# A two-layer backbone with 32 experts per layer: experts without split operands, and two gathers moved behind a loop

## The chip, the cores and the metric

The kernel runs on one core of a Trainium2 chip. The metric is the device time of one execution in microseconds; the time of a kernel is the median of its runs. The engines are TensorE (PE; its weight loads are listed as PEld), VectorE (DVE), ScalarE (ACT), GpSimd (POOL) and SyncE (SP), and 16 DMA engines serve the core.

## The reference

Two layers work on 512 latent rows and 256 context rows of 1024 floats. Each layer is a trunk (modulated norm, four mixers, output projection) and a mixture of experts over the rows; the second layer's mixture has only the 512 latent rows. All is fp32. The mixture, cut to what matters:

```python
def hier_moe(h, w_grp, b_grp, w_exp, b_exp, w_gate, w_up, w_down):
    ...  # group by the largest group logit, two experts inside it: gates, expert_id
    def expert_block(args):
        xb, e = args
        return (jax.nn.silu(xb @ w_gate[e]) * (xb @ w_up[e])) @ w_down[e]
    y_buf = lax.map(expert_block, (x_buf, blk_expert)).reshape(cap, d)
    ...
    y = y_buf[dest].reshape(n_tok, TOP_K_INNER, d).astype(jnp.float32) * gates[..., None]
    return jnp.sum(y, axis=1).astype(h.dtype)
```

A row goes to 2 of 32 experts. An expert has gate and up weights of 1024 x 512 and down weights of 512 x 1024: 2.1 MB each, 6.29 MB in all.

## The kernel before

Both layers run trunk, route, experts, in that order. The route ranks the experts by their number of rows; rank r has a fixed width `CAP[l][r]` of 24 to 128 rows, and what exceeds the widths goes through an overflow loop (`overflow`, a `For_i` at L1550 with a count that is read on the chip). Ranks 0 and 1 are fixed experts, whose weights are loaded during the route. The others are known only after it: SP reads the expert's number into a register and issues the loads of its weights with it (L148, by way of `unit2`).

**Slots.** Weights lie in slots of one unit, 128 x 1024 floats or 0.5 MB. Gate, up and down take four units each. `self.slots` holds 24 slots: a ring of 6 (`u`) and the halves of 9 double tiles (`xa`, `xb`, `xc`). Two neighbouring free slots of one double tile are filled by one load of 1 MB, others by two of 0.5 MB. `load()` issues the next loads in order as long as enough slots are free; it is called after every stage. Near the end of a layer, at the last split, the eight tiles of the split ring join the slots.

**Stages.** `seq` is the order of the products: gate (`g`), up (`u`) or both at once (`gu`) of expert e, then down (`d`) of expert e - 1. Three forms exist by width W:

- W over 64 ("many"): each unit is split into `hi` (a copy rounded to fp32r on ACT, L170) and `lo` (the difference, on DVE, L176) in rings of four tiles each, and every product is three fp32r passes on the full array (`mm3`, L195 to L197). The rows and the hidden part are split likewise. The unit's slot is given back after its split (`prep`, `done_with`), one stage ahead of the product.
- W of 33 to 64 (`gate_up2` L1403, `down2` L1458): plain fp32 in two column tiles of 64 of the array ("halves"), gate on one and up on the other.
- W up to 32 (`gate_up4` L1426, `down4` L1448): plain fp32 in four column tiles of 32 ("quarters").

In both of the last the slots are given back after the product. `rows` (L1382) transposes an expert's rows, `hT`, `hT1` and `hT4` the hidden part. `order` interleaves wide and narrow experts by `COST`; the four last ranks come at the end, and their result is added through a small product per 128 rows (`tailw`, L1839) and not scattered.

**Head of the expert stretch.** After the route POOL issues three gathers of rows (L1744, into three buffers `xb`), then a small memset that holds back the first splits (`mk`, L1757 to L1762), then the overflow loop follows, and behind it `rows(0)` and the loads of the dynamic experts.

**Widths in their order before.** Layer 0: 96 96 32 128 128 64 64 128 64 56 104 56 96 56 56 80 56 80 48 48 80 48 80 48 48 72 40 72 and four of 32. Layer 1: 96 96 32 32 96 32 96 32 88 24 80 24 72 24 72 24 72 56 56 48 48, six of 40, 72 and four of 32. So layer 0 has four experts over 96 rows, nine of 65 to 96, fourteen of 33 to 64 and five of up to 32; layer 1 has none, ten, ten and twelve.

Of the kernel before, what the change touches and what calls it, by code (L numbers as in the profile page):

```python
# [17 lines left out]
D = 1024  # L18
# [40 lines left out]
XU = ((6, 4, 8), (6, 10, 2))  # L59
# [5 lines left out]

QW = 32

COST = (19, 13, 8)
# [27 lines left out]
class K:  # L96
# [1276 lines left out]
    def xt_tile(self, l, mp, i):  # L1373
        return mp.tile([128, max(D, 8 * max(CAP[l]))], F32R, tag=f"XT{i}", name=self.nm("XT"), bufs=2)

    def rows(self, l, mp, X, W, few):
# [6 lines left out]
        v = ps.rearrange("p (k n) -> p k n", k=8)[:, :, 0:W]  # L1383
        xt = [self.xt_tile(l, mp, i)[:, 0:8 * W].rearrange("p (k t) -> p k t", k=8) for i in range(1 if few else 2)]
        if few:
            xt = xt[0].bitcast(F32)
            nc.vector.tensor_copy(xt, v)  # L1387
        else:
            nc.scalar.activation(xt[0], v, AF.Copy)
            nc.vector.tensor_sub(xt[1], v, xt[0].bitcast(F32))  # L1390
        return xt

    def halves(self, W):

        ps = self.pss("halves")
        return [ps[64 * j:64 * j + W, :] for j in range(2)]

    def gate_up2(self, xt, wg, wu):
        ps = self.halves(xt.shape[2])
        for k in range(8):  # L1400
            for j, w in enumerate((wg, wu)):
                n = w[0].shape[1]
                self.nc.tensor.matmul(ps[j], xt[:, k, :], w[k // n][:, k % n, :], start=(k == 0), stop=(k == 7),  # L1403
                                      tile_position=(0, 64 * j))
        return ps

    def hT1(self, mp, h):
        nc = self.nc
        W = h.shape[0]
        pt = self.pss("hT")  # L1410
        hv = h.rearrange("p (f k) -> p f k", k=4)
        for k in range(4):
            nc.tensor.transpose(pt[:, k * W:(k + 1) * W], hv[:, :, k], self.ident[0:W, 0:W])
        o = mp.tile([128, 2 * FE], F32R, tag="ey", name=self.nm("ehT"), bufs=3).bitcast(F32)[:, 0:4 * W]
        nc.vector.tensor_copy(o, pt[:, 0:4 * W])
        return o.rearrange("p (k t) -> p k t", k=4)

    def gate_up4(self, xt, wg, wu):

        ps = self.pss("quarters")[:, 0:256]  # L1420
        for k in range(8):
            for j, w in enumerate((wg, wu)):
                n = w[0].shape[1]
                for i in range(2):
                    a = 64 * j + 32 * i
                    self.nc.tensor.matmul(ps[a:a + 32, :], xt[:, k, :], w[k // n][:, k % n, 256 * i:256 * i + 256],  # L1426
                                          start=(k == 0), stop=(k == 7), tile_position=(0, a))
        return ps[0:64, :], ps[64:128, :]

    def hT4(self, mp, h):  # L1430
        nc = self.nc
        pt = self.pss("hT")[0:64, 0:256]
        hv = h.rearrange("p (f k) -> p f k", k=4)
        for k in range(4):
            nc.tensor.transpose(pt[:, k * 64:(k + 1) * 64], hv[:, :, k], self.ident[0:64, 0:64])
        o = mp.tile([128, 2 * FE], F32R, tag="ey", name=self.nm("ehT"), bufs=3).bitcast(F32)[:, 0:128]
        o = o.rearrange("p (k t) -> p k t", k=4)
        pv = pt.rearrange("p (k i t) -> p k i t", k=4, i=2)
        for i in range(2):
            nc.vector.tensor_copy(o[64 * i:64 * i + 64], pv[:, :, i, :])  # L1440
        return o

    def down4(self, ht, ws):
        ps = self.pss("quarters")[:, 0:256]
        for k in range(4):
            n = ws[0].shape[1]
            for j in range(4):
                self.lastm = self.nc.tensor.matmul(ps[32 * j:32 * j + 32, :], ht[:, k, :],  # L1448
                                                   ws[k // n][:, k % n, 256 * j:256 * j + 256], start=(k == 0),
                                                   stop=(k == 3), tile_position=(0, 32 * j))  # L1450
        return [ps[32 * j:32 * j + 32, :] for j in range(4)]

    def down2(self, ht, ws):
        py = self.halves(ht.shape[2])
        for k in range(4):
            n = ws[0].shape[1]
            for j in range(2):
                self.lastm = self.nc.tensor.matmul(py[j], ht[:, k, :], ws[k // n][:, k % n, j * 512:(j + 1) * 512],  # L1458
                                                   start=(k == 0), stop=(k == 3), tile_position=(0, 64 * j))
        return py  # L1460

    def gate_up(self, xt, ws):
        W = xt[0].shape[2]
        ps = self.pss("gate_up")
        for k in range(8):
            self.mm3(ps[0:W, :], (xt[0][:, k, :], xt[1][:, k, :]), self.row(ws, k), k == 0, k == 7)
        return ps[0:W, :]

    def hidden(self, mp, pg):
        h = mp.tile([128, FE], F32, tag="eh", name=self.nm("eh"), bufs=2)[0:pg.shape[0], 0:pg.shape[1]]  # L1470
        self.lasta = self.nc.scalar.activation(h, pg, AF.Silu)  # L1471
        return h

    def hT(self, mp, h):
        nc = self.nc
        W = h.shape[0]
        pt = self.pss("hT")
        hv = h.rearrange("p (f k) -> p f k", k=4)
        for k in range(4):
            nc.tensor.transpose(pt[:, k * W:(k + 1) * W], hv[:, :, k], self.ident[0:W, 0:W])  # L1480
        o = mp.tile([128, 2 * FE], F32R, tag="ey", name=self.nm("ehT"), bufs=3)
        f = [o[:, i * FE:i * FE + 4 * W] for i in range(2)]
        ht = [x.rearrange("p (k t) -> p k t", k=4) for x in f]
        nc.scalar.activation(f[0], pt[:, 0:4 * W], AF.Copy)
        nc.vector.tensor_sub(f[1], pt[:, 0:4 * W], f[0].bitcast(F32))
        return ht

    def down(self, ht, ws):
        W = ht[0].shape[2]
        py = [self.pss("down") for _ in range(2)]  # L1490
        for k in range(4):
            for n in range(2):
                self.mm3(py[n][0:W, :], (ht[0][:, k, :], ht[1][:, k, :]),
                         [x[:, n * 512:(n + 1) * 512] for x in self.row(ws, k)], k == 0, k == 3)
        return [p[0:W, :] for p in py]

    def rows_out(self, mp, py, g2, W):

        y = mp.tile([128, D], F32, tag="ey", name=self.nm("ey"), bufs=3)[0:W, :]
        n = D // len(py)  # L1500
        for i, (p, a) in enumerate(py):
            c = slice(i * n, (i + 1) * n)
            if g2 is None:
                self.nc.scalar.copy(y[:, c], p[0:W, :])  # L1504
            else:
                self.nc.vector.tensor_mul(y[:, c], p[0:W, :], g2[a:a + W, c])
        return y

    def tail_rows(self, py, j, Gs, Yr):

        a = slice(32 * j, 32 * j + 32)
        for n, (p, _) in enumerate(py):
            c = slice(n * 256, (n + 1) * 256)
            self.lastv = self.nc.vector.tensor_mul(Yr[a, c], p, Gs[a, c])
# [18 lines left out]
    def overflow(self, l, R, src, pp, mp):  # L1533
# [5 lines left out]
        raw, o, X, om = (self.xt_tile(l, mp, i % 2).bitcast(F32)[:, 0:D] for i in range(4))  # L1539
# [87 lines left out]
    def moe(self, l):  # L1627
# [23 lines left out]
        F0 = next(r for r in range(NE) if CAP[l][r] <= HW)  # L1651
        many, few = list(range(2, F0)), list(range(F0, NE))
        order = [0, 1]
        last = few[-NTL:]
        todo = [many, [r for r in few[:-NTL] if CAP[l][r] > QW], [r for r in few[:-NTL] if CAP[l][r] <= QW]]
        mean = sum(COST[i] * len(x) for i, x in enumerate(todo)) / (NE - 2 - NTL)
        ahead = COST[0] - mean
        while any(todo):
            i = next(i for i in ((2, 1, 0) if ahead > 0 else (0, 1, 2)) if todo[i])
            order.append(todo[i].pop(0))  # L1660
            ahead += COST[i] - mean
        order += last
        cap = [CAP[l][r] for r in order]
        few = [w <= HW for w in cap]
        tiny = [w <= QW for w in cap]

        seq = [("g", 0), ("u", 0)]
# [86 lines left out]
        for e in range(3):  # L1754
            gather(e)
# [249 lines left out]
```

## Time and profile before

| | us |
|---|---|
| median of 3 runs | 1918.69 |
| lowest to highest | 1917.55 to 1920.36 |
| profiled execution | 1926.93 |
| its span in the trace | 1925.1 |

The profiled execution is one more execution, with the profiler on. Times in the trace count from the start of its span. The expert stretch of layer 0 runs from about 484 to 1050 us, that of layer 1 from about 1376 to the end. A DMA share is the mean busy share of the 16 DMA engines in a stretch, PEclk the granted clock of TensorE as a share of its full 2.4 GHz; 0.50 is 1.2 GHz.

### The profile page before, as it was taken

What the parts mean: (1) busy time and instruction counts of PE and PEld (TensorE: products, weight loads), DVE (VectorE), ACT (ScalarE), POOL (GpSimd) and SP (SyncE); (2) the same over time, 40 slices, a digit from 0 to 9 for tenths busy, and PEclk for the clock granted to TensorE, in tenths of its full rate; (3) what the DMA queues carried; (4) which work ended last, traced back from release to release, by engine and by line L of the source; (5) the groups of instructions that cost most, each with busy time, mean ns of one, the idle gap of its engine ahead of it and who ended that gap; (6) DMA issues with size and microseconds to landing.
All of it is one profiled execution on the core that took longest, in us unless ns stands there. A gap on an engine that the chain in (4) does not pass through costs nothing.

```text
span 1925.1 us, 29963 instructions
## 1 busy us (share of the span) xinstructions
PE 1721.4 (89%) x11336; PEld 1113.1 (58%) x11336; DVE 1019.4 (53%) x1776; ACT 741.8 (39%) x1097; POOL 260.4 (14%) x271
## 2 busy tenths in 40 slices
PE   6999999997799999999985999999599888988866
PEld 3788688876575444444442788777466554433331
DVE  3666366546773453443526665764576565422325
ACT  4443364323573343342522564732354443200211
POOL 1000100123111111010010001011322111110010
PEclk9999999998799999999986999999699898999986
DMA  8358865453899999999997324336499999999995
GB/s 310 95 195 280 277 231 188 163 203 154 277 394 382 385 394 391 396 397 386 390 351 300 118 74 148 102 117 259 140 339 377 398 405 396 404 399 403 417 414 222
DMA packets 159605, 561.71 MB, mean 292 GB/s; under 512 B 19810, under 2 KB 46498, under 8 KB 123744
## 3 DMA queue, kind: packets, MB, share of 16 engines
q1 hardware_dynamic: 133840, 499.67, 68.8%
q0 software_dynamic: 21440, 54.16, 8.1%
q10 hardware_dynamic: 4176, 5.91, 0.9%
q8 instruction: 91, 1.49, 0.3%
q14 instruction: 58, 0.48, 0.1%
HBM read 533.54 MB, written 35.52 MB: 296 GB/s over the span
## 4 chain that ended last, share of the span: by engine, by line
DMA 26%; PE 18%; DVE 3%; issue 2%; ACT 1%; POOL 1%; SPq 0%; DVEq 0%; ACTq 0%; POOLq 0%
DMA u<-in_w_up 6%; DMA xb<-in_w_up 4%; DMA xb<-in_w_down 3%; DMA xb<-in_w_gate 3%; DMA u<-in_w_down 2%; DMA xa<-in_w_down 2%; PE zunits L195 2%; PE zunits L196 2%; PE zunits L197 2%; DMA h2d<-h 2%; PE quarters L1426 1%; DMA xa<-in_w_up 1%; PE tailw L1839 1%; PE transP L839 1%; DMA u<-in_w_gate 1%
## 5 line engine op out<-in xcount | busy, mean ns | idle before, releaser
L196 PE MATMUL gate_up<-lo,XT 128*96 128x512 f32 (+5 forms) x368 | 151.5, 412 | 7.6 <-DVE lo L176 7.2
L195 PE MATMUL gate_up<-hi,XT 128*96 128x512 f32 (+5 forms) x368 | 150.1, 408 | 8.9 <-ACT hi L170 8.1
L176 DVE TENSOR_TENSOR lo<-u,hi 128x1024 fp32r<-128x1024 f32 (+1 forms) x100 | 121.2, 1219 | 59.5 <-ACT hi L170 56.4
L197 PE MATMUL gate_up<-hi,XT 128*96 128x512 f32 (+5 forms) x368 | 149.2, 405 | 2.1 <-DVE XT L1390 2.1
L170 ACT ACTIVATE hi<-u 128x1024 fp32r<-128x1024 f32 (+1 forms) x102 | 105.6, 1044 | 106.1 <-PE zunits L196 52.3
L195 PE MATMUL zunits<-hT,hi 128*128 128x512 f32 (+1 forms) x384 | 140.3, 366 | 0.9 <-ACT cqs L689 0.8
L196 PE MATMUL zunits<-hT,hi 128*128 128x512 f32 (+1 forms) x384 | 136.2, 355 | 0.1
L1744 POOL DMA_INDIRECT xb<-h2d,tok x64 | 68.8, 1076 | 493.1 <-PE xTw L1382 468.4
L197 PE MATMUL zunits<-hT,lo 128*128 128x512 f32 (+1 forms) x384 | 135.3, 352 | 0.0
L176 DVE TENSOR_TENSOR lo<-xb,hi 128x1024 fp32r<-128x1024 f32 x100 | 118.6, 1221 | 25.1 <-ACT hi L170 24.1
L1810 POOL DMA_INDIRECT yd<-ey,dst x56 | 71.1, 1270 | 351.8 <-ACT ey L1504 171.7
L176 DVE TENSOR_TENSOR lo<-xa,hi 128x1024 fp32r<-128x1024 f32 x86 | 101.8, 1220 | 27.2 <-ACT hi L170 26.4
L170 ACT ACTIVATE hi<-xb 128x1024 fp32r<-128x1024 f32 x100 | 101.9, 1053 | 32.0 <-PE gate_up L197 28.6
L1387 DVE COPY XT<-xTw 128x256 f32<-128x256 f32 (+4 forms) x41 | 20.9, 511 | 173.5 <-PE halves L1403 105.9
L170 ACT ACTIVATE hi<-xa 128x1024 fp32r<-128x1024 f32 x86 | 87.5, 1053 | 32.0 <-DMA xa<-in_w_down 11.0
L1382 PEld LDWEIGHTS xTw<-cpack,xb 32*128 32x128 f32 (+10 forms) x512 | 64.1, 201 | 60.6 <-issue 26.7
L1382 PE MATMUL xTw<-cpack,xb 32*128 32x32 f32 (+10 forms) x512 | 72.0, 283 | 26.8 <-DVEq L1550 8.2
L1471 ACT ACTIVATE eh<-halves 56x512 f32<-56x512 f32 (+3 forms) x24 | 14.2, 591 | 207.0 <-PE halves L1403 207.0
L196 PE MATMUL down<-lo,ehT 128*96 128x512 f32 (+5 forms) x184 | 80.5, 437 | 7.3 <-DVE lo L176 6.7
L195 PE MATMUL down<-hi,ehT 128*96 128x512 f32 (+5 forms) x184 | 70.4, 444 | 16.1 <-ACT hi L170 16.1
L195 PEld LDWEIGHTS gate_up<-hi,XT 128*96 128x96 f32 (+5 forms) x368 | 59.8, 163 | 42.8 <-ACT hi L170 12.7
L196 PEld LDWEIGHTS gate_up<-lo,XT 128*96 128x96 f32 (+5 forms) x368 | 59.7, 162 | 42.6 <-DVE lo L176 17.2
(441 smaller groups left out, 3740.1 us busy)
## 6 DMA issues: line engine op xcount, KB each, us to landing
xb<-in_w_down SPq DMA_DIRECT2D x52, 1024.0 KB
xb<-in_w_up SPq DMA_DIRECT2D x50, 1024.0 KB
u<-in_w_ada SPq DMA_DIRECT2D x96, 512.0 KB
u<-in_w_up SPq DMA_DIRECT2D x91, 512.0 KB
xa<-in_w_down SPq DMA_DIRECT2D x40, 1024.0 KB
xb<-in_w_gate SPq DMA_DIRECT2D x36, 1024.0 KB
xa<-in_w_gate SPq DMA_DIRECT2D x35, 1024.0 KB
u<-in_w_gate SPq DMA_DIRECT2D x58, 512.0 KB
```

What stands on the lines that cost most here:

```text
L170: self.nc.scalar.activation(h, v, AF.Copy)
L176: self.nc.vector.tensor_sub(o, v, h.bitcast(F32))
L195: mm(out, a[0], b[0], start=start, stop=False)
L196: mm(out, a[0], b[1], start=False, stop=False)
L197: self.lastm = mm(out, a[1], b[0], start=False, stop=stop)
L839: nc.tensor.transpose(ps[:, c - a:c - a + 128], p[:, c:c + 128], self.ident)
L1382: nc.tensor.transpose(ps[:, k * 128:k * 128 + W], Xv[:, :, k], self.ident[0:W, 0:W])
L1387: nc.vector.tensor_copy(xt, v)
L1426: self.nc.tensor.matmul(ps[a:a + 32, :], xt[:, k, :], w[k // n][:, k % n, 256 * i:256 * i + 256], start=(k == 0), stop=(k == 7), tile_posi ...
L1744: self.lastp = nc.gpsimd.indirect_dma_start(out=X[e][0:cap[e], :], out_offset=None, in_=self.h2d[l][:, :], in_offset=bass.IndirectOffsetOn ...
L1810: nc.gpsimd.indirect_dma_start(out=self.yd[l][:, :], in_=y, in_offset=None, out_offset=bass.IndirectOffsetOnAxis(ap=R["dst"][0:cap[e], ord ...
L1839: nc.tensor.matmul(ps[:, c], self.G[:, t * 128:(t + 1) * 128], Yr[:, c], start=True, stop=True)
```

## The change

- No operand of an expert is split. `parts(W)` gives the parts of the rows: up to 32 one on quarters, 33 to 64 one on halves, 65 to 96 one of 64 on halves and one of 32 on quarters, 97 to 128 two of 64 on halves. `products` runs, for each k, the matmuls of all parts in turn: two for a part on halves, four for one on quarters. All are plain fp32.
- The eight `hi`/`lo` tiles are slots from the start, and since the second row tile (`XT`) goes there is room for ten double tiles instead of nine: 6 + 20 + 8 = 34 slots.
- Gate and up of every expert are loaded together (eight units), and slots are given back only after the product.
- One gather stands ahead of the overflow loop; gathers 1 and 2 follow it. The overflow takes the buffers of gathers 1 and 2 for two of its tiles. The memset, the hold and `prep` go.
- `COST` has four classes, and the order is made anew. Layer 0: 96 96 32 128 64 64 128 64 56 56 128 56 56 104 56 48 48 96 48 80 48 80 48 80 40 80 72 72 and four of 32. Layer 1: 96 96 32 32 32 96 32 96 24 88 24 80 24 72 24 72 56 56 48 48, six of 40, 72 72 and four of 32.

```diff
-XU = ((6, 4, 8), (6, 10, 2))
+XU = ((6, 4, 10), (6, 10, 4))
...
-COST = (19, 13, 8)
+COST = (24, 19, 13, 8)
...
+    def parts(W):
+
+        n = -(-W // QW)
+        return {1: [(0, QW)], 2: [(0, W)], 3: [(0, HW), (HW, QW)], 4: [(0, HW), (HW, HW)]}[n]
+
+    def streams(self, ps, n, w, ws):
+
+
+        m = 2 if w > QW else 4
+        c = n // m
+        o = []
+        for j in range(m):
+            b = 128 // m * j
+            x, f = divmod(c * j, n // len(ws))
+            o.append((ps[b:b + w, 0:c], b, ws[x], slice(f, f + c)))
+        return o
+
+    def products(self, x, parts, ws, n, K, name):
+
+
+        S, out = [], []
+        for a, w in parts:
+            ps = self.pss(name)
+            st = self.streams(ps, n, w, ws)
+            S += [(a, w) + y for y in st]
+            out.append((ps, [y[0] for y in st]))
+        for k in range(K):
+            for a, w, o, b, m, c in S:
+                q = m[0].shape[1]
+                self.lastm = self.nc.tensor.matmul(o, x[:, k, a:a + w], m[k // q][:, k % q, c], start=(k == 0),
+                                                   stop=(k == K - 1), tile_position=(0, b))
+        return out
+
+    def gate_up(self, mp, xt, parts, wg, wu):
+
+
         nc = self.nc
...
+        h = mp.tile([128, FE], F32, tag="eh", name=self.nm("eh"), bufs=2)
+        H = []
+        for i, ((a, w), (ps, _)) in enumerate(zip(parts, self.products(xt, parts, (wg, wu), 2 * FE, 8, "gate_up"))):
+            c = FE if w > QW else FE // 2
+            r = w if w > QW else HW
+            v = h[64 * i:64 * i + r, 0:c]
+            self.lasta = nc.scalar.activation(v, ps[0:r, 0:c], AF.Silu)
+            self.lastv = nc.vector.tensor_mul(v, v, ps[64:64 + r, 0:c])
+            H.append(v)
+        return h, H
...
+        self.slots += [[self.hp.tile([128, U], F32R, tag=x, name=self.nm("u")).bitcast(F32), False, None]
+                       for x in ("hi", "lo") for _ in range(4)]
...
-        seq = [("g", 0), ("u", 0)]
+        seq = [("gu", 0)]
         for e in range(1, NE):
-            seq += ([("gu", e)] if few[e] else [("g", e), ("u", e)]) + [("d", e - 1)]
+            seq += [("gu", e), ("d", e - 1)]
...
-        for e in range(3):
-            gather(e)
-
-        mk = [pp.tile([1, 1], F32, name=f"mk{l}_{i}") for i in range(2)]
-        with tc.issue_after(self.lastp.ins):
-            nc.gpsimd.memset(mk[0], 0.0)
-        self.hold = self.laste, nc.vector.tensor_copy(mk[1], mk[0])
-        prep(0)
-        self.hold = None
-        self.overflow(l, R, src, pp, mp)
+        gather(0)
+        self.overflow(l, R, src, pp, mp, XB[1:])
+        gather(1)
+        gather(2)
...
-            prep(i + 1)
...
+            if m == "gu":
+                h[e] = self.gate_up(mp, xt.pop(e), parts[e], *raw.pop((m, e)))
+                done_with(i)
...
+                py = self.down(ht.pop(e), parts[e], *raw.pop((m, e)))
+                done_with(i)
```

## Rows read from the trace of the kernel before

**Rows 1.** The page: busy time of the engines; DMA share in 40 slices.
```profile
PE 1721.4 (89%) x11336; PEld 1113.1 (58%) x11336; DVE 1019.4 (53%) x1776; ACT 741.8 (39%) x1097; POOL 260.4 (14%) x271
...
DMA  8358865453899999999997324336499999999995
```

**Rows 2.** Chain of waits, end of layer 1: start, us, what (merged).
```profile
1893.05 10.86 DMA u<-in_w_down
...
1903.95 1.12 PE quarters L1448 x8
```

**Rows 3.** Windows: us, busy by engine (count), PEclk, DMA share, GB/s.
```profile
494.30:530.00 35.70, 34.33 (x153) 24.15 (x155) 27.33 (x26) 23.37 (x26) 4.39 (x3) 0.90 0.89 309
530.00:970.00 440.00, 416.38 (x1936) 222.34 (x1930) 206.05 (x237) 186.30 (x236) 52.57 (x52) 0.98 1.01 390
...
990.00:1000.00 10.00, 9.48 (x45) 3.90 (x46) 0.00 (x0) 0.00 (x0) 3.23 (x6) 0.67 0.54 186
...
1387.00:1430.00 43.00, 41.47 (x226) 27.96 (x225) 32.53 (x33) 24.46 (x28) 7.97 (x5) 0.90 0.90 310
...
1480.00:1880.00 400.00, 346.28 (x2020) 165.92 (x2018) 172.67 (x247) 100.89 (x121) 55.85 (x50) 0.93 1.01 405
```

**Rows 4.** Timeline around both overflow loops: start, us, what [idle before, releaser].
```profile
494.32 1.30 SPq L148 DMA_DIRECT2D u<-in_w_gate  x2
...
1377.03 1.03 POOL L1744 DMA_INDIRECT xb<-h2d,tok  x1 [9.65 <-DVE nb L1272]
...
1379.64 0.91 POOL L1744 DMA_INDIRECT xb<-h2d,tok  x1 [0.30 <-issue]
...
1384.65 4.61 DVE L176 TENSOR_TENSOR lo<-xb,hi 128x1024 fp32r<-128x1024 f32 x4
1384.73 2.50 PE L1382 MATMUL xTw<-cpack,xb 96*128 96x96 f32 x14 [7.78 <-issue]
...
1387.02 0.35 SPq L148 DMA_DIRECT2D xb<-in_w_gate  x1
```

**Rows 5.** Timeline of TensorE: the first tail expert of layer 0.
```profile
985.06 0.62 PE L1426 MATMUL quarters<-xb,XT 128*32 128x256 f32 x4
```

**Rows 6.** Line 1550, the loop: durations in ns, first and last start in us.
```profile
L1550 DVEq EVENT_SEMAPHORE  x26: 21/50/119, 492.9 to 1384.3; - x26
L1550 POOLq EVENT_SEMAPHORE  x24: 42/43/140, 491.8 to 1384.2; - x24
```

**Rows 7.** Timeline of TensorE, full array to halves to quarters.
```profile
966.62 0.40 PE L196 MATMUL gate_up<-lo,XT 128*72 128x512 f32 x1
966.86 0.40 PE L197 MATMUL gate_up<-hi,XT 128*72 128x512 f32 x1
967.18 1.92 PE L1458 MATMUL halves<-xc,ehT 128*40 128x512 f32 x8
968.93 1.89 PE L1458 MATMUL halves<-u,ehT 128*40 128x512 f32 x8
970.75 0.63 PE L1426 MATMUL quarters<-u,XT 128*32 128x256 f32 x4
```

**Rows 8.** Stages: chain of waits; groups by form (530 to 970; 1480 to 1880).
```profile
971.38 0.63 PE hT L1480 x4
...
1415.14 0.99 PE xTw L1382 x8
...
1421.81 3.59 PE quarters L1426 x64
...
L1351 PE MATMUL tail_place<-cpack,teq 128*128 128x128 f32 x24 | 4.1, 295 | 0.8 <-DVE teq L1346 0.8
...
L1448 PE MATMUL quarters<-xb,ehT 128*32 128x256 f32 x224 | 14.0, 383 | 2.7 <-DMA xb<-in_w_down 2.7
```

**Rows 9.** Waits of TensorE, 530 to 970: us in total, times, longest.
```profile
PE gate_up L195 <- ACT hi L170: 8.1, 4, 2.2
...
PE down L196 <- DVE lo L176: 5.1, 9, 0.9
```

More of the change, by code (lines that the diff above doesn't have):

```diff
@@ L1370, in tail_scale, with xt_tile, rows @@
         return o
-    def xt_tile(self, l, mp, i):
-        return mp.tile([128, max(D, 8 * max(CAP[l]))], F32R, tag=f"XT{i}", name=self.nm("XT"), bufs=2)
-    def rows(self, l, mp, X, W, few):
+    def xt_tile(self, mp):
+        return mp.tile([128, D], F32, tag="XT", name=self.nm("XT"), bufs=2)
+    def rows(self, mp, X, W):
         nc = self.nc
@@ L1391, in rows @@
-        return xt
[L1393 to L1405, printed above, removed]
@@ L1407, in hT1 @@
-    def hT1(self, mp, h):
-        nc = self.nc
-        W = h.shape[0]
-        pt = self.pss("hT")
[L1411 to L1428, printed above, removed]
@@ L1443, in down4 @@
[L1443 to L1451, printed above, removed]
@@ L1453, in down2 @@
[L1453 to L1497, printed above, removed]
-        y = mp.tile([128, D], F32, tag="ey", name=self.nm("ey"), bufs=3)[0:W, :]
[L1500 to L1506, printed above, removed]
+        xt = self.xt_tile(mp)[:, 0:8 * W].rearrange("p (k t) -> p k t", k=8)
@@ new lines, in hT @@
+    def hT(self, mp, h, parts):
+        nc = self.nc
+        h, H = h
+        pt = self.pss("hT")
+        W = parts[-1][0] + parts[-1][1]
+        o = mp.tile([128, D], F32, tag="ey", name=self.nm("ehT"), bufs=3)[:, 0:4 * W]
+        o = o.rearrange("p (k t) -> p k t", k=4)
+        if len(parts) == 2 and W == 128:
+            H, parts = [h], [(0, 128)]
+        for i, ((a, w), v) in enumerate(zip(parts, H)):
+            hv = v.rearrange("p (f k) -> p f k", k=4)
+            r, n = hv.shape[0:2]
+            p = pt[0:n, 256 * i:256 * i + 4 * r]
+            for k in range(4):
+                nc.tensor.transpose(p[:, k * r:(k + 1) * r], hv[:, :, k], self.ident[64 * i:64 * i + r, 64 * i:64 * i + r])
+            if n == 128:
+                nc.vector.tensor_copy(o[:, :, a:a + w], p.rearrange("p (k t) -> p k t", k=4))
+            else:
+                pv = p.rearrange("p (k i t) -> p k i t", k=4, i=2)
+                for j in range(2):
+                    nc.vector.tensor_copy(o[64 * j:64 * j + 64, :, a:a + w], pv[:, :, j, :])
+        return o
@@ new lines, in down, with rows_out @@
+    def down(self, ht, parts, ws):
+        return [x[1] for x in self.products(ht, parts, (ws,), D, 4, "down")]
+    def rows_out(self, mp, py, parts, g2, W):
+        y = mp.tile([128, D], F32, tag="ey", name=self.nm("ey"), bufs=3)[0:W, :]
+        for (a, w), ps in zip(parts, py):
+            w = min(w, W - a)
+            n = D // len(ps)
+            for i, p in enumerate(ps):
+                c = slice(i * n, (i + 1) * n)
+                b = 128 // len(ps) * i
+                if g2 is None:
+                    self.nc.scalar.copy(y[a:a + w, c], p[0:w, :])
+                else:
+                    self.nc.vector.tensor_mul(y[a:a + w, c], p[0:w, :], g2[b:b + w, c])
@@ L1538, in overflow @@
         NB = 2 * T
-        raw, o, X, om = (self.xt_tile(l, mp, i % 2).bitcast(F32)[:, 0:D] for i in range(4))
+        raw, o, X, om = self.xt_tile(mp), self.xt_tile(mp), *XB
         g2, xs, sc = (mp.tile([128, D], F32, tag="ey", name=self.nm("ov"), bufs=3) for _ in range(3))
@@ L1714, in done_with @@
                 x[1] = False
-        def prep(i):
-            if i < len(seq):
-                m, e = seq[i]
-                Wt[m, e] = raw.pop((m, e))
-                if not few[e]:
-                    Wt[m, e] = self.splits(Wt[m, e][0])
-                    done_with(i)
-        xt, h, ht, pg, X, written = {}, {}, {}, {}, {}, []
-        last_split = max(i for i, (m, e) in enumerate(seq) if not few[e])
+        xt, h, ht, X, written = {}, {}, {}, {}, []
         load(2)
@@ L1775, in moe @@
         for i, (m, e) in enumerate(seq):
[L1776 to L1795 removed]
+            if m == "gu":
+                h[e] = self.gate_up(mp, xt.pop(e), parts[e], *raw.pop((m, e)))
+                done_with(i)
+                if e > 0:
+                    ht[e - 1] = self.hT(mp, h.pop(e - 1), parts[e - 1])
                 rows(e + 1)
```

77 lines of the change are left out of this document (17 added, 60 removed).

## The prediction

> **What bounds the kernel now.** I read the page first: TensorE is busy 89% of the span and the DMA engines 9 tenths or more in every slice of both expert stretches, so the page alone does not tell which of the two holds the end [rows 1]. The chain of waits does, for layer 1: late in it stand weight loads, and the last expert's product starts right where a down load has landed, at 1903.95 us [rows 2]. For layer 0 the windows say the same. So the MoE of each layer is a fixed number of weight bytes drained at a fixed rate: in the steady part 390 GB/s in layer 0 and 405 in layer 1, at a DMA share of 1.01 in both [rows 3]. The head of each stretch falls short: 309 GB/s over 35.7 us and 310 over 43 us [rows 3]. At the steady rates the same bytes would have taken 35.7 x 309/390 = 28.3 us and 43 x 310/405 = 32.9 us, so the heads lose **7.4 and 10.1 us**. By the shares, .11 x 35.7 = 3.9 us and .10 x 43 = 4.3 us of that are idle DMA engines; the rest (3.5 and 5.8) is slow transport. What starts the head is the overflow loop: the first weight load of a dynamic expert is issued just after it, at 494.32 and at 1387.02 [rows 4]. TensorE is the near second: the last product before the four tail experts ends at 985.06 in layer 0 [rows 5].
>
> **The change, part by part.**
>
> **Earlier start.** One gather instead of three stands ahead of the loop. In layer 1 the third is issued at 1379.64, 2.61 us after the first (1377.03). POOL's first wait on the loop's semaphores stands at 491.8 in layer 0, later than its gathers were issued, so the loop waits for gathers to land [rows 4, 6]; one gather lands about 2.6 us before three do. In layer 0 DVE came to the loop later still, at 492.9, held by three split subtractions, which go: the gate becomes POOL at 491.8 - 2.6 = 489.2, so 492.9 - 489.2 = 3.7 us, and the first load moves from 494.32 to 490.6. In layer 1 TensorE passes at 1384.73, and would at 1382.1; the first load waited there for the splits that began at 1384.65 and now waits for nothing: 1387.02 becomes 1382.1, **4.9 us** earlier [rows 4, 6]. The two gathers moved behind the loop are two instructions on POOL's queue with nothing ahead of them; expert 1's rows are wanted only after expert 0's first product, some 13 us on. If that cover were gone, one landing would be exposed (about 4 us).
>
> **Products without splits.** At full clock, and with two records to a matmul, 16 records in halves take 970.75 - 967.18 = 3.57 us [rows 7], so a halves down costs 3.57 and a gate-and-up of 32 records 7.14. A gate-and-up in quarters takes 3.59 and a down 14.0 / 7 = 2.0 [rows 8]. The unsplit form costs 72 passes .234 us apart, 16.8 us per expert. A 97 to 128 row expert becomes two halves parts: 2 x (7.14 + 3.57) = 21.4. A 65 to 96 row expert runs two halves and four quarters in turn inside each k, and so changes the array's tiling twice per k. The trace has such changes singly [rows 7]: passes of one kind start .23 to .24 us apart, the full-array pass ahead of the halves .32, so .09 for the change; of the halves, the first eight records take 1.75 us and the second, up to the quarters, 1.82, where four pairs at .43 make 1.72, so .03 for the first pass in a new tiling and .10 for leaving it. I take **.12 us per change**: 16 in gate-and-up and 8 in down, 2.9 us per expert. Whether one that comes every few passes costs as much as one between stages no row shows. Zero bounds it below, if the next part's start hides in the last; above I take twice it, .24, if the wait ahead of a change and the one behind it are both paid each time. The nearest row is the single change, so .12. The expert is then 7.14 + 3.59 + 3.57 + 2.0 + 2.9 = 19.2, with transposes of rows (.99) and of the hidden part in two groups (about 1.2) 21.4 us, against 16.8 + .99 + .63 = 18.4 now; the two-halves one is 23.0.
>
> The trace agrees here with a rule that speaks against this part. The Trainium skill, "TensorEngine Tiling (Array Packing)", section "Tiling Modes", says that a change of tiling mode, unlike a change of tile, drains TensorE. The Trainium skill, "TensorE: Matmul & The Clock Gate", section "Single matmul latency", puts a drain at about 175 ns; as an estimate from that page, 24 changes would cost 4.2 us per expert, and the forecast would move toward rival A below; the rows' .12 gives 2.9.
>
> Where does that extra work go? Layer 0 has nine such experts and four of over 96 rows, layer 1 ten and none: 9 x 3.0 + 4 x 4.6 = 45 us more TensorE in layer 0. Against it go the waits for splits, of which the two largest between 530 and 970 are 8.1 and 5.1 us [rows 9], the stretched passes behind them, and the idle in that stretch: TensorE is busy 416.4 of 440 us [rows 3]. Summed anew, the 28 experts ahead of the tail cost 9 x 21.4 + 4 x 23.0 + 14 x 12.4 (halves: 7.14 + 3.57 + .99 + .63) + 6.9 (one in quarters) + 8 (tail tables: twice 4.1, for their two kinds of passes [rows 8]) = 473 us. Not all of the 23.6 us of idle was for splits; I keep 5 (bounds: none, and 23.6 - 13.2 = 10.4). The first product starts at about 492.3 (row transposes at half clock and their copy after the loop), and costs 2 us more while the granted clock, .90 over both heads [rows 3], is still at half. So the 28 end at 492.3 + 2 + 473 + 5 = **972**, 13 us before the 985.06 of now [rows 5]: DMA keeps the end, with little to spare. In layer 1 twelve experts are in quarters (6.9 us against some 16 us of loading each), and TensorE stays far under. Dropping the split copies frees ACT and DVE, which set no end; only the waits named count. The second row copy, silu and multiply per mixed expert lie beside the next 12 us of products.
>
> **Slots and holes.** A slot was given back after its split, now after the product. SP's only work there is the loads, so what is queued behind such a wait is loads alone. Ahead stand ten free slots, 5.2 MB: 13.4 us at 390 GB/s. Loads from 490.6 stop at 504.0; expert 0's gate-and-up (7.14 + 3.59 + 1.9 = 12.6, plus 2 us while the clock is at half) ends at 492.3 + 14.4 = 506.7: hole 2.7. Eight slots come back (4.2 MB, 10.8 us), to 517.5; expert 1's ends 506.7 + .8 + 12.4 = 519.9: 2.4. A third, smaller one follows the 128-row expert (about 1.5): 6.6, with a little latency **6.9 us** for 3.9 now. Layer 1 alike: 1382.1 + 13.2 = 1395.3 against 1384.3 + 14.4 = 1398.7, 3.4; then 2.6 and 1.9: **7.9** for 4.3. The 34 slots (24 before, 32 near the end) are what makes the holes end there.
>
> **Slow transport.** With several loads queued instead of one slot at a time, I let most of the 3.5 us in layer 0 (3.0) and most of the 5.8 in layer 1 (4.0) go; the gathers and scatters beside them stay. Bounds: nothing, and all. More slots that are not neighbours (eight loose ones more) turn 1 MB loads into 0.5 MB ones; no row prices the difference; I take 1 us a layer, within 0 and 2.
>
> **Sum.** Layer 0: -3.7 + (6.9 - 3.9) - 3.0 + 1.0 = -2.7. Layer 1: -4.9 + (7.9 - 4.3) - 4.0 + 1.0 = -4.3. Together -7.0: the profiled 1926.93 becomes 1919.9, and that execution lay 8.24 above the median of 1918.69, so **1911.7 us**. With the bounds of slow transport and loose loads the forecast's own range is 1906 to 1917.
>
> **Rivals.**
> **A. Slower: changes of tiling cost double.** At .24 a mixed expert takes 24.3, nine add 26 us: TensorE ends the 28 at 998, 13 us past 985.06. Two slots more than now have at that point cover 2.7 of it, and the DMA hole near the end of layer 0 (its share is .54 between 990 and 1000 [rows 3]) another 4.6: +5.7 there. In layer 1 DMA still bounds, but the holes grow by 1.9 + 1.9 + 1 and eat the gain: +.5. Total 1918.7 + 6.2 = **1925**. It decides from about .2 per change, where the 13 us and the slots are used up. For it: the price at a change every pass is not in the trace, and the margin is thin. Against: the single changes read .09 to .13.
> **B. No change.** The slow transport is due to the other queues and stays whole: layer 0 is then -3.7 + 3.0 + 1.0 = +.3, layer 1 -4.9 + 3.6 + 1.0 = -.3, so **1918.7**: the early start pays just for the deeper holes. For it: the gathers that land in the head are the same ones. Against: by rate over share the head moves 309 / .89 = 347 GB/s while it moves, the steady part 386 [rows 3], with gathers and scatters in both.
> **C. Larger gain: the changes hide.** Holes shrink by 1.9, 1.9 and 1 us in each layer, and TensorE ends the 28 experts at 946: -7.0 - 9.6 = -16.6, **1902**. For it: the two column groups overlap in steady runs. Against: every row with a change shows it paid.
>
> **How the numbers follow.** Forecast 0.43, A 0.21, B 0.20, C 0.16. A measurement of this kernel tells about 0.2% (3.8 us) from no change. Faster by more than that: most of the forecast (.37) and C, with a little of B (.02): .55; within: the rest of the forecast (.06), most of B (.17) and .02 of A: .25; slower: the rest of A and .01 of B: .20. The range reaches from a little below C to a little above A: 1900 to 1928.
>
> **What would show it.** Of the changed kernel: first dynamic loads near 490.6 and 1382.1; three holes in DMA's share in the first 45 us of each stretch, 6 to 8 us in all; a mixed gate-and-up of 12.6 us (10.7 if the changes hide, 14.6 if they cost double); DMA share 1.0 through layer 0 until past 980. I would be wrong if TensorE's chain, not the weights, closes layer 0; if the loop opens no earlier, because something other than the gathers holds it; or if the trace shows the mixed stage at a cost outside 0 to .24 per change.

## The result

The changed kernel takes 1940.17 us (median; 1937.65 to 1942.48) beside 1918.55 us for the kernel before: a ratio of 1.0111 with an interval of 1.0094 to 1.0129, so **slower by 1.1%** where 1911.7 was forecast. Its profiled execution took 1937.65 us, with a span of 1935.9.

Cut at the first gather of each layer's experts and at the first product of each layer's tail (`tailw`), the two profiled executions compare like this:

| us | before | after | difference |
|---|---|---|---|
| start to first gather of layer 0 | 485.7 | 478.8 | -6.9 |
| experts of layer 0, to the first `tailw` | 563.2 | 589.2 | **+26.0** |
| from there to the first gather of layer 1 | 328.2 | 326.1 | -2.1 |
| experts of layer 1, to the first `tailw` | 529.0 | 523.9 | **-5.1** |
| the rest | 19.1 | 17.9 | -1.2 |

The first line is no effect of the change: in the twelve kernels of the experiments, two of them the kernel before with one edit in its expert stretch, the first gather stood at 478.8 to 482.5. It is most of the 8.24 us by which the profiled execution of before lay above its median. The changed kernel's profiled execution in turn lay 2.5 us below its median. So the spans differ by 10.8 us, but the kernels by 21.6; layer 1 went as forecast, within the scatter (a kernel below whose layer 1 is the same, `e3_g2`, took 527.2 us there, 3.3 more), and layer 0 lost 26 us.

Windows of the changed kernel: the head of both stretches, the middle and the end of layer 0, the steady part of layer 1 (columns as in [rows 3]):

```profile
484.70:530.00 45.30, 44.01 (x354) 15.08 (x352) 6.60 (x11) 4.55 (x10) 7.69 (x8) 0.93 0.99 359
...
540.00:960.00 420.00, 413.45 (x2233) 146.94 (x2229) 60.64 (x120) 59.04 (x116) 45.19 (x47) 1.00 0.99 382
...
960.00:1030.00 70.00, 63.15 (x528) 22.64 (x524) 8.45 (x22) 10.83 (x24) 8.32 (x13) 0.85 0.61 223
...
1000.00:1010.00 10.00, 10.00 (x38) 3.62 (x30) 0.85 (x2) 0.38 (x1) 0.00 (x0) 0.50 0.01 2
...
1399.80:1443.00 43.20, 41.78 (x332) 14.70 (x336) 8.35 (x16) 1.93 (x4) 6.52 (x7) 0.93 0.99 352
...
1497.00:1893.00 396.00, 367.83 (x2550) 128.29 (x2546) 99.61 (x214) 17.43 (x36) 42.50 (x47) 0.98 1.01 400
```

The heads are better than before, at a share of .99 where [rows 3] had .89 and .90. In the middle of layer 0 TensorE is busy 413.45 of 420 us and sets the pace: the queue of the loads waits for slots that its products still hold (waits of SP, 495 to 1030: us in total, times, longest).

```profile
SPq L147 <- PE down L1416: 78.8, 31, 26.7
SPq L147 <- PE gate_up L1416: 76.8, 32, 9.6
```

Between 960 and 1030 the DMA share is .61, so .39 x 70 = 27 us without a load; the same window of the kernel before has .94, 4 us:

```profile
960.00:1030.00 70.00, 51.96 (x403) 24.25 (x405) 28.19 (x39) 14.30 (x19) 8.44 (x14) 0.78 0.94 369
```

That hole, 23 us more than before, is most of the loss of layer 0. The slower middle, 382 GB/s for 390, costs another 420 x 8/390 = 8.6 us, and the earlier start and the better head give back some 6.

Two places of TensorE's timeline show where its time goes. First two experts of 96 and of 80 rows, whose gate-and-up has 96 records each:

```profile
503.85 6.38 PE L1416 MATMUL gate_up<-xa,XT 128*64 128x512 f32 x48 [0.24 <-DVE XT L1383]
510.17 6.38 PE L1416 MATMUL gate_up<-xb,XT 128*64 128x512 f32 x48
516.48 0.69 PE L1450 MATMUL hT<-cpack,eh 64*128 64x64 f32 x4
...
876.70 1.63 PE L1416 MATMUL gate_up<-u,XT 128*64 128x512 f32 x6
878.26 0.68 PE L1450 MATMUL hT<-cpack,eh 48*128 48x48 f32 x4
878.87 6.36 PE L1416 MATMUL gate_up<-u,XT 128*64 128x512 f32 x42
885.16 7.92 PE L1416 MATMUL gate_up<-xa,XT 128*64 128x512 f32 x48
```

The first takes 516.48 - 503.85 = **12.63 us**, the 12.6 of the forecast. The second takes 1.56 up to the transposes and 893.01 - 878.87 = 14.14 behind them: **15.70 us** for the same records. Its first six records (two on halves, four on quarters) are one weight's matmuls of the first k; the other weight's six come behind the transposes. A group of six alone takes 1.56 us, one of twelve, with gate and up side by side on their column tiles, 1.58. Where gate and up of a k stand apart, the k costs twice; here that happens at two of eight k. Seven of the nine mixed experts of layer 0 are cut like this (14.17 us with one k parted, 15.65 to 15.70 with two), one ran in part at half clock (14.62), and the mean of all nine is 15.07 us. (Stage times here and below go from the start of each record to that of the next, summed over a product's records, without idle time.)

Second, the end of layer 0, on TensorE:

```profile
986.77 0.60 PE L1416 MATMUL gate_up<-u,XT 128*32 128x256 f32 x4
...
988.89 1.93 PE L1416 MATMUL gate_up<-u,XT 128*32 128x256 f32 x32
996.70 2.07 PE L1366 MATMUL tail_scalew<-u,gr 1*128 1x512 f32 x2 [5.87 <-DMA u<-modd]
...
1004.42 3.78 PE L1366 MATMUL tail_scalew<-u,gr 1*128 1x512 f32 x4
...
1008.93 1.12 PE L1416 MATMUL down<-xa,ehT 128*64 128x512 f32 x2
...
1017.22 0.60 PE L1416 MATMUL gate_up<-xa,XT 128*32 128x256 f32 x4
```
and GpSimd's timeline at the same time:

```profile
989.41 0.95 POOL L1744 DMA_INDIRECT yd<-ey,dst  x1 [23.34 <-ACT ey L1473]
990.35 1.26 POOL L301 DMA_DIRECT2D u<-modd  x2
```

The broadcast of the two scale rows (`u<-modd`) stands on POOL's queue behind the scatter of the last but one ordinary expert, which had to wait for that expert's down product; the scale products wait 5.87 us for it; and the last ordinary down product, queued behind them, starts at 1008.93 and ends at 1017.22, at half clock in part (granted .50 between 1000 and 1010). Its weights and those of the first tail expert hold slots until then. (In the kernel before the scale products began at 990.52, behind the last ordinary down.) The queue of the loads shows it (waits of SP, 960 to 1030: us in total, times, longest):

```profile
SPq L147 <- PE down L1416: 37.2, 9, 26.7
SPq L147 <- PE gate_up L1416: 19.6, 5, 9.6
```

### The profile page after: what moved, and what is told of

Its sections match the earlier page's. It is cut to its first block, busy times and chain, and to the rows that moved or that the text cites. A ratio compares the mean times of both kernels' runs of the same rounds, so it can differ in the third digit from the quotient of the medians.

```text
span 1935.9 us, 32616 instructions
## 1 busy us (share of the span) xinstructions
PE 1778.4 (92%) x12876; PEld 973.3 (50%) x12876; DVE 740.0 (38%) x1599; ACT 466.8 (24%) x842; POOL 234.3 (12%) x267
## 5 line engine op out<-in xcount | busy, mean ns | idle before, releaser
L1416 PE MATMUL gate_up<-u,XT 128*32 128x256 f32 (+4 forms) x1664 | 287.6, 493 | 5.9 <-DMA u<-in_w_up 4.1
L1416 PE MATMUL gate_up<-xb,XT 128*32 128x256 f32 (+4 forms) x1152 | 224.4, 489 | 10.4 <-DMA xb<-in_w_up 9.1
L1416 PE MATMUL gate_up<-xa,XT 128*32 128x256 f32 (+4 forms) x680 | 156.9, 490 | 8.6 <-DMA xa<-in_w_up 8.4
L1416 PEld LDWEIGHTS gate_up<-u,XT 128*32 128x32 f32 (+4 forms) x1664 | 82.6, 121 | 160.7 <-issue 134.6
L1416 PE MATMUL gate_up<-xc,XT 128*32 128x256 f32 (+4 forms) x440 | 127.3, 498 | 2.8 <-DMA xc<-in_w_up 2.1
L1416 PE MATMUL down<-u,ehT 128*32 128x256 f32 (+4 forms) x656 | 111.6, 514 | 7.0 <-DMA u<-in_w_down 6.1
L1416 PE MATMUL down<-xb,ehT 128*32 128x256 f32 (+4 forms) x592 | 96.4, 498 | 2.6 <-DMA xb<-in_w_down 2.4
L1381 PE MATMUL xTw<-cpack,xb 96*128 96x96 f32 (+6 forms) x512 | 72.9, 282 | 20.4 <-DVE XT L1383 8.7
L1381 PEld LDWEIGHTS xTw<-cpack,xb 96*128 96x128 f32 (+6 forms) x512 | 63.1, 201 | 55.0 <-issue 24.0
L175 DVE TENSOR_TENSOR lo<-u,hi 128x1024 fp32r<-128x1024 f32 (+2 forms) x54 | 65.6, 1217 | 46.6 <-ACT hi L169 44.1
```

What stands on the lines that cost most here:

```text
L175: self.nc.vector.tensor_sub(o, v, h.bitcast(F32))
L1416: self.lastm = self.nc.tensor.matmul(o, x[:, k, a:a + w], m[k // q][:, k % q, c], start=(k == 0), stop=(k == K - 1), tile_position=(0, b))
```

## The experiments

Every kernel ran beside the kernel before; the ratio is to that, with its interval. A time given as "about" is the ratio times the 1918.55 us of the result; the kernel before took 1921.4 to 1922.8 us in these runs, so a median measured here lies some 4 us higher than such a time. "Hole" is the time without loads between 960 and 1030 us, from the DMA share of that window (27 us in the changed kernel, 4 before).

**Parts one after another** (`e1_seq`): each product runs all k of the halves, then all k of the quarters.

```diff
-        for k in range(K):
-            for a, w, o, b, m, c in S:
+        for p, _ in parts:
+            for k in range(K):
+                for a, w, o, b, m, c in S:
+                    if a == p:
```

> The changed kernel, but a 65 to 96 row expert runs all its k on halves first and then all its k on quarters: one change of tiling per product instead of two per k. Theory 1 (TensorE closes layer 0, because alternating makes the mixed products dear: 15.07 us mean for gate-and-up and 6.86 for down): they fall to about 10.8 and 5.6, TensorE gains some 9 x 5.5 = 50 us in layer 0, DMA holds the end again, and the time is about 1911 us. Theory 2 (the stop at the end of layer 0, where the scale rows of the tail come late, is what costs): the products get cheaper all the same, but the DMA hole near 970 to 1020 stays for the most part, and the time is about 1925.

Measured: 0.9994 (0.9983 to 1.0006), about 1917; hole 18 us. One of the nine mixed gate-and-ups fell to 10.6 us:

```profile
502.68 3.65 PE L1418 MATMUL gate_up<-xa,XT 128*64 128x512 f32 x16
506.17 3.60 PE L1418 MATMUL gate_up<-xb,XT 128*64 128x512 f32 x16
509.70 1.93 PE L1418 MATMUL gate_up<-xa,XT 128*32 128x256 f32 x32
511.45 1.91 PE L1418 MATMUL gate_up<-xb,XT 128*32 128x256 f32 x32
513.29 0.69 PE L1452 MATMUL hT<-cpack,eh 64*128 64x64 f32 x4
```

The first, at half clock in part, took 12.0, and the other seven 13.5 to 14.0, because TensorE's queue mixed halves and quarters and parted gate and up all the same: the written order isn't the queued one. The means are 13.1 and 6.1 us. The cheaper products give the 22 us back, and the hole stays for two thirds. Both theories hold a part.

**Held order** (`e2_fixed`): each matmul is queued behind the one written before it.

```diff
-                self.lastm = self.nc.tensor.matmul(o, ...
+                with self.tc.issue_after(self.lastm.ins):
+                    self.lastm = self.nc.tensor.matmul(o, ...
```

> The changed kernel, with the matmuls of every product held to the order in which they are written, so that gate and up of one k always stand side by side. Theory 1a (the alternation itself costs as forecast, .12 to .14 us per change, and the rest comes from gate and up of a k standing apart in TensorE's queue): gate-and-up of mixed experts takes 12.6 us everywhere instead of 15.7, down 6.3, TensorE gains about 27 us in layer 0, and the time is about 1920. Theory 1b (they stand apart because the up weights land later, so that holding the order only turns the extra passes into waits): the stage is 15 us or more with idle in it, and the time stays at 1940.

Measured: 1.0021 (1.0009 to 1.0033), about 1923; hole 20 us. The mixed gate-and-up takes 12.63 us where nothing cuts in and 13.6 where transposes do, mean 13.51, without idle time in it. So the parting was a matter of the queue's order and not of late weights: theory 1a.

**Scale rows early** (`e3_g2`): the broadcast is issued three experts earlier.

```diff
+                    if j == -4 and l == 0:
+                        gs = [self.bc(self.buf(True), l, 3, m) for m in range(2)]
                     if j == -1:
                         ...
-                            g2 = [self.bc(self.buf(True), l, 3, m) for m in range(2)]
+                            g2 = gs
```

> The changed kernel, with the two scale rows of layer 0's tail broadcast three experts earlier (two slots fewer for that time). Theory 2: the 5.9 us wait of the tail's scale product and the half clock behind it go, loads flow again some 10 to 15 us sooner, and the time is about 1926 to 1930. Theory 1: TensorE is late already, only the wait itself goes, and the time is about 1934. If the rows were not late because of GpSimd's queue: 1940.

Measured: 1.0044 (1.0028 to 1.0061), about 1927; hole 17.5 us. The scale products wait no longer and run at full clock, and 13 of the 22 us are back. They still stand ahead of the last ordinary down.

**Scale products behind the last ordinary down** (`e9_tail`), with the early rows:

```diff
                     if j == -1:
+                        self.endm = self.lastm
...
+                with self.tc.issue_after(self.endm.ins):
                     self.nc.tensor.matmul(ps[:, c], self.gr[:, 128 * m:128 * m + 128], g[0:1, c], ...
```

> The changed kernel, with layer 0's two scale rows broadcast three experts earlier and the tail's scale products held behind the last ordinary down product (they stood ahead of it). If the order at the end of layer 0 costs by itself, the last ordinary down follows the first tail expert's gate-and-up at once: it ends some 9 us sooner than with the early broadcast alone (which gave 1932 us), the DMA hole there, 17 us wide in that kernel, shrinks by as much, and the time is 1922 to 1924. If TensorE's lateness alone makes the hole: 1932 again.

Measured: 1.0028 (1.0015 to 1.0042), about 1924; hole 10.5 us. Counted from the layer's first gather, the last ordinary down starts after 514.7 us instead of 520.4; first the kernel with the early rows alone, then this one:

```profile
1001.65 7.80 PE L1416 MATMUL down<-xa,ehT 128*64 128x512 f32 x48
...
993.44 6.38 PE L1417 MATMUL down<-xa,ehT 128*64 128x512 f32 x48
```

It ends 7 us sooner where 9 was forecast. In the time that is 3 us beside the early rows alone, where 8 to 10 had been forecast, and the two intervals overlap: the order's own share is seen in the trace and in the hole, and is not clear of the noise in the time. Both edits together are worth 16 us.

**Both, without and with the held order** (`e10_seq_tail`, `e11_seqfix_tail`):

> Both edits: parts one after another, and the tail of layer 0 in the other order with its scale rows early. If the two causes are separate and add: from 1918 (parts in sequence alone, with 18 us of DMA hole near 975 to 1010) the time falls by some 13 to 15 us, to about 1904, faster than both kernels. If the hole comes from slots that are given back late and not from the order: 1915 to 1918.

> As the one with both edits, and the matmuls of each product held to their written order. If gate and up of a k standing apart still costs something with the parts in sequence (13.6 us of gate-and-up where 10.6 was clean): the stage falls to about 10.6 and TensorE gains some 20 us in layer 0; the time falls only where TensorE still held the end, to about 1901 to 1904. If the held order makes TensorE wait for loads instead: as without it, or slower.

Measured: 0.9948 (0.993 to 0.9965), about 1909, and **0.9896 (0.988 to 0.9913)**, about 1899 (1902.27 us as measured beside 1922.28). The first gains 9 us on the parts in sequence, where 13 to 15 had been forecast. In layer 0 the causes add: from the 589.2 us of its experts the sequence alone takes 18, the tail's edits alone 13, both 30. In the whole time it is 22 and 16 alone and 31 together. The last kernel beats both. Its mixed gate-and-up has a mean of 11.3 us (11.7 with the waits for loads in it), and in its windows of layer 0 the loads never stop:

```profile
540.00:960.00 420.00, 405.74 (x2434) 162.00 (x2430) 63.81 (x127) 63.53 (x125) 48.37 (x52) 0.98 1.01 389
...
960.00:1010.00 50.00, 34.20 (x328) 15.04 (x324) 19.18 (x31) 8.11 (x13) 6.22 (x10) 0.74 1.02 414
```

Experts of layer 0 take 554.2 us in it and those of layer 1 522.1 (before: 563.2 and 529.0).

**Only the alternation back** (`e14_fix_tail`): held order and tail as above, but halves and quarters in turn inside each k.

> The changed kernel's alternation of halves and quarters inside each k, with the held order and the tail in the other order; so beside the fastest kernel only the alternation is back. Gate-and-up of mixed experts 12.6 to 13.6 us instead of 11.3, down 6.5 instead of 5.6: some 9 x 2.8 = 25 us of TensorE time in layer 0. If TensorE is the bound with it (rival A of the prediction): a DMA hole comes back near 970 and the time is 1910 to 1915. If loads still cover it: 1902 to 1904, and the forecast would have held had the order been kept.

Measured: 0.9937 (0.9913 to 0.9961), about 1906 (1911.88 as measured); hole 6 us, and experts of layer 0 at 561.1 us. So TensorE closes layer 0 even with the order kept. Beside the fastest kernel that is some 8 us more, by intervals that just touch. Mixed gate-and-up 13.50, down 6.56: the price of the alternation is 13.50 + 6.56 - 11.32 - 5.64 = 3.1 us per mixed expert, and 7 us of the layer.

**Two parts on halves** (`e4_two_halves`): `3: [(0, HW), (HW, HW)]` in `parts`.

> The changed kernel, with experts of 65 to 96 rows as two parts on halves (the second padded to 64), so that no product changes the tiling. Theory 1 (the changes are what makes the mixed products dear): gate-and-up 13.9 us and down 6.9, against means of 15.07 and 6.86: 7 us of TensorE time in layer 0, and a time of about 1933, although a quarter more columns run through the array. If the changes were hidden: some 9 x 4.6 = 41 us more than two parts side by side would take, and a time above 1945.

Measured: 1.0118 (1.0102 to 1.0135), about 1941: like the changed kernel itself, not 7 us better. Mixed gate-and-up takes 14.2 us and down 7.6, together 21.8 as against 15.07 + 6.86 = 21.9. Running a quarter more columns costs about what the changes of tiling and the parted order do together. The tail's order was left as in the changed kernel.

**One gather ahead in the kernel before** (`e6_before_one_gather`): the gathers of experts 1 and 2 written behind the overflow loop.

> The kernel before, with only the first gather ahead of the overflow loop and the other two behind it; splits, order and slots as they were. If one gather less per step opens the loop 2.6 us sooner in each layer: the first dynamic load is issued 2.6 us earlier after the route in both layers and the time is 1913 to 1915. If something other than the gathers holds the loop: 1918.5.

Measured: 0.9993 (0.9979 to 1.0008). The edit did not do what it was written for: in layer 0 GpSimd's queue had all three ahead of the loop again (480.24 and 482.52 beside 478.89, the loop left at 487.8), in layer 1 two. In the changed kernel the loop itself writes the buffers of the other two, which keeps them behind it. So the question was put the other way round.

**Two more gathers ahead** (`e13_more_gathers`), on the fastest kernel:

> The fastest kernel so far (parts in sequence, held order, tail in the other order; 1902 us, ratio 0.990), with two more gathers ahead of the overflow loop (rows of expert 0 into the buffers of experts 1 and 2, gathered again behind it), so three ahead as in the kernel before. If the loop waits for every gather ahead of it: the first dynamic load comes 2.6 us later in each layer (8.5 instead of 5.9 us after the first gather) and, since loads set the end in both layers, the time rises by about 5 us, to 1907. If the loop is held by something else: 1902.

Measured: 0.9931 (0.9908 to 0.9954), some 6.7 us more than without, though the two intervals overlap a little. Timeline of this kernel around the loop of layer 0:

```profile
480.49 1.04 POOL L1708 DMA_INDIRECT xb<-h2d,tok  x1 [12.28 <-DVE nb L1271]
481.84 0.98 POOL L1720 DMA_INDIRECT xb<-h2d,tok  x1 [0.30 <-issue]
483.12 0.96 POOL L1720 DMA_INDIRECT xb<-h2d,tok  x1 [0.31 <-issue]
...
488.83 1.55 PE L1382 MATMUL xTw<-cpack,xb 96*128 96x96 f32 x8 [8.48 <-SPq L1674]
...
489.34 0.36 SPq L147 DMA_DIRECT2D xc<-in_w_gate  x1
```

The first dynamic load comes 8.9 and 8.6 us after the first gather, against 5.9 and 5.9 in the fastest kernel: 3.0 and 2.7 us for two gathers. So the loop opens later for each gather ahead of it. What it waits for is not shown. GpSimd is busy 1.3 us with issuing each of them, which alone makes 2.6, and in six kernels, with one, two or three ahead, the first product behind the loop starts 3.4 to 5.3 us after the last of them was issued. Whether that stretch is the landing or the loop's own start no run separates. Besides, the two gathers added here write buffers that the loop uses. In the kernel before the loop doesn't use them, and three gathers show a like effect: that product starts 7.7 to 8.1 us after the first gather, against 5.4 to 6.0 with one in the changed and the fastest kernel.

**Fewer slots** (`e15_fewer_slots`): the fastest kernel without the eight slots in the split tiles.

> The fastest kernel without the eight slots that lie in the split tiles: 26 slots instead of 34. If the depth is needed because slots come back only after the products: holes of the DMA engines in layer 0, some 2 to 5 us at its head and more near its end, and 1908 to 1914 us. If slots come back one by one while a product runs, so that 26 are enough: 1902.

Measured: 0.9955 (0.994 to 0.997). Its windows show both sides of the eight slots:

```profile
490.00:500.00 10.00, 10.00 (x85) 3.75 (x84) 0.69 (x1) 0.59 (x1) 0.00 (x0) 0.92 0.38 115
...
540.00:960.00 420.00, 402.87 (x2384) 159.01 (x2384) 63.21 (x126) 61.61 (x121) 48.20 (x51) 1.00 1.01 393
```

That is about 1910. With two free slots ahead instead of ten there is a hole of 6 us at the head. In the steady part of layer 0, at the same share, 26 slots move 393 GB/s and 34 move 389. But the alternation brought back, with 34 slots and as many loads of 0.5 MB, moves 393 as well:

```profile
540.00:960.00 420.00, 412.35 (x2326) 147.69 (x2321) 60.76 (x121) 63.03 (x124) 47.43 (x50) 1.00 1.01 393
```

So in layer 0 the loose slots are not shown to cost anything. In layer 1 it looks otherwise: over 380 us of its steady part every kernel with 34 slots moves 400 to 402 GB/s, and the four with 24 or 26 move 404. Between 1480 and 1840 us the changed kernel issues 108 loads of 0.5 MB and 77 of 1 MB, this one 62 and 104.

**The tail's edits in the kernel before** (`e16_before_tail`):

> The kernel before, with layer 0's scale rows broadcast three experts earlier and the tail's scale products behind the last ordinary down (where they stood already). The only gain to be had is its DMA hole of 4.6 us between 990 and 1000: 1914 to 1916 us if the late rows made it, 1918.5 if not. The rest of what the fastest kernel gains over the kernel before (1 percent) is then due to the change itself.

Measured: 0.9962 (0.9939 to 0.9986), about 1911, and a DMA share of .99 between 960 and 1030. So of the 1.0% that the fastest kernel gains, .4% were to be had without this change, and the change itself, with its parts in sequence and its order held, is worth the other .7%, give or take .3.

## Why the prediction was wrong

The direction and the range failed, at one step: **"So the 28 end at [...] 972, 13 us before the 985.06 of now"**, from which it followed that "DMA keeps the end". Counted from the first gather (485.7 before, 478.8 after), that step put the end of the last ordinary down at 972 - 485.7 = 486; it was 1017.2 - 478.8 = 538, 52 us later: TensorE closed layer 0, and the weights waited for it. Two terms make 51 of the 52:

- The mixed gate-and-up was sized 12.6 us, which is right where gate and up of a k are queued side by side; the mean was 15.07, 9 x 2.5 = 22 us more. Their downs took 6.86 for 6.5 (3 us), the downs on halves 3.99 for 3.57 (14 of them, 6 us).
- The order at the end of the layer was no term of the sum at all. Ahead of the last ordinary down stood the first tail expert's gate-and-up (6.2 us), the wait for the scale rows (5.9 us) and the scale products (7.6 us), in part at half clock: about 20 us.

The price per change of tiling, which the prediction doubted most, was sized .12 with bounds of 0 and .24; the difference of clean gate-and-ups gives (12.63 - 10.61) / 14 = **.14** (15 changes inside the alternating one, one in the sequence), and clean downs give (6.31 - 5.45) / 6, the same. That term was good.

The Trainium skill's rule that a change of mode drains TensorE ("TensorEngine Tiling (Array Packing)", "Tiling Modes") agrees with these stages in that every change costs; that a drain is what it costs, no run shows. The 175 ns that the Trainium skill gives for a drain ("TensorE: Matmul & The Clock Gate", "Single matmul latency"), taken in the prediction as an estimate of that price, is above the .14 measured.

Both misses have one root: I added up stage times as if the engine's queue ran one stage after the other. The trace of before showed that it doesn't. Four records of a tail expert's gate-and-up stand at 970.75, and the transposes of another expert follow them at 971.38 [rows 7, 8]: a stage cut in two. That gate-and-up is the first tail expert's, and stands ahead of the last ordinary down, which ends at 985.06; the row there [rows 5] is the second's. So the sum of 28 left out a stage that the trace of before had inside it. Stages in one tiling are cut as well and lose little by it (the gate-and-up on halves of the changed kernel: mean 7.13 us, uncut 7.02); with two tilings per k each parted k costs 1.54 us more ((15.70 - 12.63) / 2).

**Rival A** was the case that came: TensorE is the bound in layer 0. Its mechanism, changes at twice the price, wasn't: what doubled was the passes. It gave 1925, for the products alone; the held alternation with the tail mended (about 1906) and unmended (about 1923) shows that the way to 1940 is the parting and the tail. The condition that I set, 13 us and a few slots of margin, was the right quantity; the 52 us are four times as much. Even with the order held and the tail mended the last ordinary down ends 505.5 us after the first gather, 19 later than 486. **Rival C**, changes that hide, fell with the .14.

**Earlier start**: forecast -3.7 and -4.9 us to the first load; measured 8.6 to 5.9 and 10.0 to 5.8, so -2.7 and -4.2. That fewer gathers ahead open the loop sooner is shown by the run with more of them; that the loop waits for their landing, as the prediction read it, is not.

**Slots and holes**: wrong, and too dark. No hole came at the heads: 6.9 and 7.9 us had been forecast, and the share was .99. I let eight slots come back at the end of a product, but each comes back when its last record is done. In SP's timeline the load at 489.71 fills the last two of the ten free slots; the next two go out, into slots given back, while expert 0's gate-and-up (486.87 to 501.5) still runs:

```profile
489.71 0.86 SPq L147 DMA_DIRECT2D u<-in_w_gate  x2
494.11 2.56 SPq L147 DMA_DIRECT2D u<-in_w_up  x2
497.52 1.71 SPq L147 DMA_DIRECT2D u<-in_w_gate  x2
```

**Slow transport**: wrong the other way. Of 3.5 and 5.8 us I let 3.0 and 4.0 go; at .99 of the time but 359 and 352 GB/s, 45.3 x 31/390 = 3.6 and 43.2 x 53/405 = 5.7 us are still lost. Rival B had this term right.

**Loose loads**: 1 us a layer, within 0 and 2, was too little in layer 1. Its steady rate fell from 405 to 400 GB/s, 396 x 5/400 = 5 us, and the kernel with fewer slots is back at 404. In layer 0 no run shows a cost of them.

In layer 1, where TensorE has room, these three misses cancel: -4.2 for the start, 10.1 - 5.7 = -4.4 for the head, +5 for the rate make -3.6, measured -5.1, forecast -4.3; single executions scatter there by some 3 us. The right total rests partly on luck.

**Two smaller readings** of the prediction were off and changed nothing: the slices at the edges of the two stretches hold 8, 7, 4 and 5 tenths of DMA and not 9 [rows 1], and the 72 passes that it calls unsplit are those of the split form.

## What to carry to other kernels

A sum of stage times holds only for the queued order: before summing, look whether stages in the trace are cut by others, and what a cut costs in the new form. When a change moves the bound's neighbour close to the bound, go through the end of the stage, instruction by instruction, on every queue: there a late small transfer and one product behind it cost 16 us, where the dearer products of a whole layer cost 22. And price the side on which nothing was to happen: in layer 1, loads of half the size took back as much as the better head gave.

## What was not expected of the hardware

Two column tiles work at the same time only where their matmuls are neighbours in the queue: six records alone took 1.56 us, twelve from both 1.58. A change between column tilings of 64 and 32 costs about .14 us at full clock when it comes every few passes, near the .09 to .13 of the single ones [rows 7]. A loop whose count is read on the chip opened 1.3 to 1.5 us later for each of two more gathers issued ahead of it. A scale product on one row took 1.06 us a pass at the end of layer 0, where the granted clock was .50 to .65, and .59 in layer 1, where it was 1.00.

Why the queue parts gate and up of some experts and not of others, no run shows: holding the order removes it, and that is all that was tried.
